# Half 0's second-norm work queued behind the newest output-weight split, and new asking places for norms, loads and the first gate and up weights

## The chip, the cores and the metric

The kernel runs on one core of a Trainium2 chip. The metric is the device time of one execution in microseconds. Before the change it was 1154.78 us, the median of three runs (1154.27 to 1156.89). The execution that was profiled took 1155.71 us; its trace spans 1153.9 us from the first to the last instruction of the program.

## The reference

One decoder layer over 1024 positions of width 1024, in float32:

```python
h = rms_norm(x, ln_pre_mix)
proj = h @ w_in                                   # pool channels, q, k, v
q, k = rope(q, pos), rope(k, pos)
pool_out = multi_scale_pool(u_pool, w_pool, pool_scale)
attn_out = dilated_attention(q, k, v)             # 12 heads, three (window, dilation) settings
mix = concatenate([pool_out, attn_out]) @ w_out
x = x + rms_norm(mix, ln_post_mix)                # "first norm" below
h = rms_norm(x, ln_pre_ffn)                       # "second norm" below
f = (silu(h @ w_gate) * (h @ w_up)) @ w_down
x = x + rms_norm(f, ln_post_ffn)
```

where `rms_norm(x, g)` is `x * rsqrt(mean(x*x) + 1e-6) * g` over the channels.

## The kernel before

**Number format.** Activations and weights lie with channels on the 128 partitions. Every large product is made of three matmuls (`PASSES`, line 256): an operand is split into an upper part, a rounded copy, and a lower part, what is left of it; upper by upper, upper by lower and lower by upper are summed. A weight tile of 128 x 1024 is loaded into a raw tile (`wraw`, three buffers, line 235), its upper part is written by ScalarE (ACT, line 244), its lower part by VectorE (DVE) or GpSimd (POOL, two halves), line 248. `split` and `wtile` (lines 243 to 254) do this; the split tiles named `whl` have two buffers.

**Halves.** The 1024 positions are worked in two halves of 512, half 0 and half 1, written `h`.

**Stages.** Input projection, attention and the pooling mixer take the first part of the span; the output projection of half 0 is woven into the end of attention. Then come, around 440 to 560 us, the output projection of half 1, the two norms of each half, and the first gate and up products. From there on a scheme of seven products per two-by-two block carries gate and up (`seven`, line 1324), and the down projection and the last norm end the kernel.

**Who sets the order.** Matmuls run in the order in which they are written (`keep_in_program_order`). That order is made by hand: `put` (line 952) and `emit` (line 901) give each step of a list a place between a lower and an upper number, sort all steps by place, and run them. In the attention part the unit of place is one of twelve units (head pair and half); some steps also pull filler matmuls until a reckoned due time is reached (`await_`, line 488; the constants `lt`, `ls`, `lm`, `lw`). On the other engines the build's scheduler sets each engine's order from the order of writing and from its own reckoning of when operands are ready, and the engine's queue holds them in that order. `with tc.issue_after(i)` adds, for each instruction traced inside on the engine of `i`, that it must stand behind `i` in that engine's queue; it adds no wait between engines. DMA loads are issued by SyncE's queue (SP), in order.

**Half 1's output projection** (`out_proj`, line 1027) has eight output blocks d0 to d7 of 24 matmuls, 192 in all, which are the unit 0 to 1 of its `emit` (line 1215). The first seven k-tiles of d0, d1 and d2 come first (21 matmuls each), then their last k-tile (3 each), then d3 to d7 whole; banks alternate between `pj` (even d) and `s` (odd d). The weights of block d + 1 are asked at the third k-tile of block d: those of d1 at matmul 6, of d2 at 27, of d4 at 78, d5 at 102, d6 at 126, d7 at 150. d3's are asked ahead of everything, into a buffer of their own (`b`). Lower parts of d0 and d1 go to POOL, the others to DVE (line 1034). The buffer of d6's split tile is that of d4.

**A half's two norms** (`chain`, line 1149) consist of: a load of the residual, the first norm's mean (eight small matmuls with `ones`, then ACT, then POOL's power, lines 1132 to 1140 and 273), its row (four transposes, then ACT into `rb`), eight adds, eight squares, the second norm's mean, its row, and scalings:

- `add` (line 1160): two DVE instructions that make x1 in `z` (lines 1162 and 1163), an upper part by ACT (1164), a lower part by DVE (1165), and a store.
- `square` (1169): an ACT square into one of two strips `p`, and a DVE sum into `sq` (lines 1129 and 1130, shared with the first norm's squares).
- `scale` (1178): one ACT instruction on `z` (1181).

Their places are the ten numbers of `c0` (half 0) and `c1` (half 1): mean, row, adds from and to, squares from and to, second mean, second row, scalings from and to. Half 0's first five lists are emitted with half 1's output projection. All else goes with the next stretch (the `emit` at line 1448), in which one unit is 48 steps of three matmuls: the gate and up products of two feed-forward tiles with half 0, and two products of the seven-scheme. The products of the same two tiles with half 1 follow it from place 1.0, at the same 48 steps to the unit. The second tile's weights are asked there at `ew` (gate, up), and `ahead` makes sums of weight blocks on DVE (lines 1331 to 1337) and splits on POOL (1367).

Of the kernel before, what the change touches and what calls it, by code (L numbers as in the profile page):

```python
# [8 lines left out]
F32 = mybir.dt.float32  # L9
F32R = mybir.dt.float32r  # L10
AF = mybir.ActivationFunctionType
ALU = mybir.AluOpType
# [6 lines left out]
NK = 8  # L19
# [19 lines left out]
 'oq': (0, 1, 1, 1, 0, 0, 0, 1),  # L39
 'lag': 3.0,  # L40
# [109 lines left out]
 'cut': 5,  # L150
 'ew': (0.11, 0.19),
 'c1': (0.08, 0.17, 0.18, 0.8, 0.4, 0.95, 1.57, 1.7, 0.6, 0.94),
 'c2': ((0.95, 1.35), (1.4, 1.6)),
 'e0': ((0.26, 0), (0.42, 0), (0.47, 0.9)),
 'e1': (((1.08, 0), (1.28, 0), (1.3, 1.9)), ((2.0, 0), (2.01, 0), (2.02, 2.03)))}
PRM["x"] = {(0, 'm'): 5, (0, 's', 0): 8, (0, 's', 1): 6, (0, 's', 2): 5, (0, 's', 3): 3, (0, 's', 4): 2, (0, 's', 6): 3,
# [31 lines left out]
def hybrid_block(ctx: ExitStack, tc: tile.TileContext, xT, w_in, w_v, w_pin, w_pool, w_out, w_gate, w_up, w_down,  # L188
                 g1, g2, g3, g4, pscale, cost, sint, maskA, maskB, quadA, quadB, lsel, ident, perm, band, out):
    nc = tc.nc  # L190

    def mm(*a, **k):
        return tc.keep_in_program_order(nc.tensor.matmul(*a, **k))  # L193
# [9 lines left out]
    def did(key):  # L203
        seen[key] = seen.get(key, 0) + 1

    def need(key, n):
        assert seen.get(key, 0) >= n, (key, n, seen.get(key, 0))
# [8 lines left out]
    def bank(tag):  # L216
        return psum.tile([P, 512], F32, name="ps_" + tag, tag=tag)
# [9 lines left out]
    def cload(src, shape, name, pool=None, eng=nc.sync):  # L227
        t = (pool or const).tile(shape, F32, name=name)
        eng.dma_start(t, src)
        return t  # L230

    loads = []

    def raw_tile(src, own=None):
        r = own or wpool.tile([P, 1024], F32, name="wraw", tag="wraw", bufs=3)
# [5 lines left out]
        return r  # L241

    def split(dst, src, eng, pin=lambda x: x):
        nc.scalar.activation(dst[:, 0], src, AF.Copy)  # L244
        n = src.shape[-1]
        w = n if eng is nc.vector else n // 2
        for at in range(0, n, w):
            pin(eng.tensor_tensor(dst[:, 1, at:at + w], src[:, at:at + w], dst[:, 0, at:at + w].bitcast(F32), ALU.subtract))  # L248

    def wtile(src, eng=None, pool=None, tag="whl", bufs=2, raw=None, pin=lambda x: x):  # L250
        r = raw_tile(src, raw)
        w = (pool or wpool).tile([P, 2, 1024], F32R, name=tag, tag=tag, bufs=bufs)
        split(w[:, :, :r.shape[-1]], r, eng or nc.gpsimd, pin)
        return w
# [28 lines left out]
    def slot(k, shape, dt, name):  # L283

        return xgp.tile(shape, dt, name=name, tag="xk%d" % k)
# [119 lines left out]
    ls = [cload(lsel[i], [P, P], "ls%d" % i, con1) for i in range(2)]  # L405
# [616 lines left out]
    def room(h, n):  # L1022
        if h:
            return fw([P, 2, 2, 512], F32R)
        return slot((2, 3, 6, 7)[n], [P, 2, 2, 512], F32R, "m0%d" % n)

    def out_proj(h, parts, done):

        box = {}

        def weights(d):
            if d not in box:
                own = h == 1 and d == 3
                box[d] = wtile(w_out[d], nc.gpsimd if d < 2 else nc.vector,
                               *((xgp, "xk5", 1) if d == 2 else (ffnl, "b4", 1) if own else ()),
                               raw=big(5, [P, 1024], F32, "b5") if own else None)

        def step(d, k, first, last, n):
            if first and n == 0:
                weights(d)  # L1040
                box[d] = box[d], bank("s" if d % 2 else "pj")
            if k == 4 and n == 0 and d + 1 < NK:
                weights(d + 1)
            w, ps = box[d]
            if k < 2:
                need(("pool", h), 2)
            if k == 7:
                need(("v", 5, h), 2 * len(GROUPS[h]))
            mk = m[h][k // 2 - 1 if k > 1 else 3][:, k % 2]
            a, b = PASSES[n]  # L1050
            mm(ps, w[:, a, k * P:(k + 1) * P], mk[:, b], start=(first and n == 0), stop=(last and n == 2))
            if last and n == 2:
                did(("z", h, d))
                nc.scalar.activation(z[h](d), ps, AF.Copy)
                if done:
                    done(d, ps)
        ks = (2, 3, 4, 5, 0, 1, 6, 7)
        order = ([(d, k) for kk in (ks[:7], ks[7:]) for d in range(parts) for k in kk]
                 + [(d, k) for d in range(parts, NK) for k in ks])
        return [lambda a=(d, k, k == ks[0], k == ks[-1], n): step(*a) for d, k in order for n in range(3)], weights  # L1060
# [11 lines left out]
    for step, at in zip(mixed(0), G["lr"]):  # L1072
        put([step], at, 0)
    st, weights = out_proj(0, 3, None)
    for d in range(2):
        put([lambda d=d: weights(d)], G["lw0"][d], 0)
# [72 lines left out]
    def chain(h, sq, s3, at):  # L1149

        sl = slice(h * 512, (h + 1) * 512)
        x = []

        def load():
            for n in range(2):
                x.append(slot((6, 4)[h] + n, [P, 4, 512], F32, "xr%d" % n))
                with tc.issue_after(behind.ins) if h else ExitStack():
                    nc.sync.dma_start(x[n], xT[:, 4 * n:4 * n + 4, sl])

        def add(d):  # L1160
            zd, (hi, lo) = z[h](d), (t[:, d % 4] for t in block(d // 4, h))
            nc.vector.scalar_tensor_tensor(zd, zd, g2s[:, d:d + 1], sq.rb, op0=ALU.mult, op1=ALU.mult)  # L1162
            nc.vector.tensor_tensor(zd, zd, x[d // 4][:, d % 4], ALU.add)  # L1163
            nc.scalar.activation(hi, zd, AF.Copy, scale=g3s[:, d:d + 1])
            nc.vector.scalar_tensor_tensor(lo, zd, g3s[:, d:d + 1], hi.bitcast(F32), op0=ALU.mult, op1=ALU.subtract)
            nc.sync.dma_start(x1d[d, :, sl], zd)
            did(("x1", h, d))

        def square(d):
            need(("x1", h, d), 1)  # L1170
            s3.add(d, z[h](d))
            did(("s3", h, d))

        def rows():
            s3.rows(r3[:, sl])
            did(("r3", h))

        def scale(d):
            need(("s3", h, d), 1)
            did(("g3", h, d))  # L1180
            nc.scalar.activation(z[h](d), z[h](d), AF.Copy, scale=g3s[:, d:d + 1])
        return [([load], -1, 0), ([sq.mean], at[0], 0), ([sq.rows], at[1], 0),
                ([lambda d=d: add(d) for d in range(NK)], at[2], at[3]),
                ([lambda d=d: square(d) for d in range(NK)], at[4], at[5]),
                ([s3.mean], at[6], 0), ([rows], at[7], 0),
                ([lambda d=d: scale(d) for d in range(4 if h else NK)], at[8], at[9])]

    put([next_pools], G["np"], 0)
    sqs = [(Squares(), Squares(tag=("o", "pj")[h], to=eps[:, 4 * h:4 * h + 4])) for h in range(2)]
# [10 lines left out]
    def big(n, shape, dt, name):  # L1200

        return ffnl.tile(shape, dt, name=name, tag="b%d" % n)

    def block(kh, h):

        if (kh, h) not in B:
            n = {(0, 0): 0, (1, 0): 2, (1, 1): 4}.get((kh, h))
            B[kh, h] = [(fw([P, 4, 512], F32R, "fw") if n is None else big(n + i, [P, 4, 512], F32R, "b%d%d" % (kh, h)))
                        for i in range(2)]
        return B[kh, h]  # L1210

    st, weights = out_proj(1, 3, sqs[1][0].add)
    weights(3)
    first_half = chain(0, *sqs[0], G["c0"])
    emit((st, 0.0, 1.0), *first_half[:G["cut"]])
    behind = loads[-2]
# [225 lines left out]
    def next_weights(f, i):  # L1442
        with tc.issue_after(powers[-1].ins):
# [3 lines left out]
    ratio = len(beside) / len(before)  # L1447
    emit((before, 0.0, 1.0), (beside, 1.0, 1.0 + ratio), (one[2], 1.0 + ratio, 1.0 + ratio + len(one[2]) / len(before)),
         *first_half[G["cut"]:], ([lambda: let_go(kept)], G["c0"][7] + 0.001, 0), *chain(1, *sqs[1], G["c1"]),
         *(([lambda a=(f, i): next_weights(*a)], G["ew"][i], 0) for f in range(1, EARLY) for i in range(2)),  # L1450
         ([ahead], 0.1, 0), ([lambda: let_go(held)], G["c1"][7] + 0.001, 0),
# [266 lines left out]
```

## Time and profile before

| What | us |
|---|---|
| median of three runs | 1154.78 |
| profiled execution | 1155.71 |
| span of its trace | 1153.9 |
| PE (matmul) busy | 1128.3 |
| PE weight loads busy | 979.2 |
| DVE busy | 790.1 |
| POOL busy | 604.1 |
| ACT busy | 545.4 |

A row of a timeline gives the start in us from the span's start, the length, engine, line, operation, what is written and read, the shape and the count of merged instructions; the bracket gives the engine's idle time before it and what ended it. A matmul's end is modelled, and matmuls overlap, so a busy PE is not yet a PE at its peak: the distance between the starts of two blocks tells how fast they ran. "Granted clock" is the share of full clock that TensorE was given.

### The profile page before, as it was taken

The page shows a single profiled execution, that of the slowest core. Times are in us where ns is not written, and L with a number is a line of the kernel's source. Part 1 is how long each engine was busy: PE and PEld are TensorE (multiplying, and loading weights), DVE is VectorE, ACT ScalarE, POOL GpSimd, SP SyncE. Part 2 cuts the span into 40 slices and gives each one's busy share as a digit, 9 for nine tenths or more (in the row PEclk, how much of TensorE's full clock was granted, in tenths as well). Part 3 has the DMA queues.
Part 4 walks back from the last instruction along what each step waited for, and adds up shares of the span by engine and source line. Part 5 has one row for each costly group of instructions (what it writes and reads, how often), then busy time and mean ns, then how long its engine had stood idle before and what let it go on. Part 6 is the DMA issues. An engine that isn't in the chain of part 4 may idle for free.

```text
span 1153.9 us, 17223 instructions
## 1 busy us (share of the span) xinstructions
PE 1128.3 (98%) x6134; PEld 979.2 (85%) x6134; DVE 790.1 (68%) x1481; ACT 545.4 (47%) x1035; POOL 604.1 (52%) x541
## 2 busy tenths in 40 slices
PE   9999999999999999899999999999999999999996
PEld 7999999999898888778788888888888888888895
DVE  7957878787788674979467655676556365554685
ACT  7456676665677663855333222322232435443420
POOL 0103646465476222250487656876676978566521
PEclk9999999999999999999999999999999999999998
DMA  8224151515136457430344354545444869666542
GB/s 289 107 78 165 56 165 56 164 57 172 49 119 246 169 217 253 166 110 28 126 155 149 137 199 166 183 154 200 165 178 172 279 228 364 211 218 197 169 146 73
DMA packets 85797, 188.51 MB, mean 163 GB/s; under 512 B 8784, under 2 KB 24656, under 8 KB 84304
## 3 DMA queue, kind: packets, MB, share of 16 engines
q1 hardware_dynamic: 84992, 186.89, 46.7%
q8 instruction: 48, 0.79, 0.3%
q10 hardware_dynamic: 720, 0.53, 0.1%
q14 instruction: 37, 0.30, 0.1%
HBM read 134.44 MB, written 52.95 MB: 162 GB/s over the span
## 4 chain that ended last, share of the span: by engine, by line
PE 80%; DVE 9%; issue 3%; DMA 3%; ACT 2%; POOL 1%; SPq 0%; POOLq 0%; DVEq 0%; ACTq 0%
PE ps_pj L193 28%; PE ps_o L193 22%; PE ps_s L193 20%; PE ps_t L193 7%; PE ps_t L196 3%; DMA wraw<-in_w_out_dram 1%; DVE sq L1130 1%; ACT pp L678 1%; DVE z L1162 1%; DMA b<-in_w_out_dram 1%; DVE z L1163 1%; DVE pp L675 1%; DVE tT L1291 1%; DMA xraw<-in_xT_dram 1%; DMA wraw<-in_w_gate_dram 1%
## 5 line engine op out<-in xcount | busy, mean ns | idle before, releaser
L193 PE MATMUL ps_pj<-x,whl 128*128 128x512 f32 x480 | 143.1, 410 | 0.0
L1367 POOL TENSOR_TENSOR fw<-rw,fw 128x512 fp32r<-128x512 f32 x74 | 101.6, 1398 | 65.2 <-ACT fw L1365 63.8
L248 POOL TENSOR_TENSOR whl<-wraw,whl 128x512 fp32r<-128x512 f32 x50 | 66.6, 1353 | 121.6 <-ACT whl L244 121.6
L193 PE MATMUL ps_o<-tT,fw 128*128 128x512 f32 x504 | 117.7, 389 | 0.0
L193 PEld LDWEIGHTS ps_o<-tT,fw 128*128 128x128 f32 x504 | 94.5, 188 | 19.9 <-DVE sq L1402 0.3
L730 POOL TENSOR_SCALAR pp<-pp,wv 128x256 f32<-128x256 f32 (+1 forms) x156 | 72.8, 486 | 72.4 <-DVE wv L714 63.7
L678 ACT ACTIVATE pp<-pp,sx 128x128 f32<-128x128 f32 (+1 forms) x192 | 89.4, 468 | 34.9 <-DVE sx L675 34.1
L193 PEld LDWEIGHTS ps_pj<-x,whl 128*128 128x128 f32 x480 | 85.7, 191 | 9.4
L1367 POOL TENSOR_TENSOR whl<-rw,whl 128x512 fp32r<-128x512 f32 x42 | 59.9, 1449 | 60.4 <-ACT whl L1365 55.5
L1365 ACT ACTIVATE fw<-rw 128x1024 fp32r<-128x1024 f32 x37 | 38.5, 1056 | 94.3 <-DVE rw L1333 43.0
L193 PE MATMUL ps_pj<-whl,x 128*128 128x256 f32 x528 | 81.0, 293 | 0.0
L1514 POOL TENSOR_TENSOR op<-rw,op 128x512 fp32r<-128x512 f32 x38 | 60.2, 1584 | 37.1 <-ACT op L1513 34.9
L1513 ACT ACTIVATE op<-rw 128x1024 fp32r<-128x1024 f32 x38 | 40.2, 1060 | 65.2 <-PE ps_t L193 30.2
L193 PEld LDWEIGHTS ps_pj<-whl,x 128*128 128x128 f32 x528 | 70.3, 196 | 0.1
L776 DVE TENSOR_TENSOR ptr<-ps_t,ptr 128x512 fp32r<-128x512 f32 (+1 forms) x84 | 55.9, 665 | 16.4 <-ACT ptr L775 15.9
L450 POOL TENSOR_TENSOR rsw<-rsw,sinr 128x512 f32<-128x512 f32 x20 | 26.3, 1316 | 70.9 <-DVE rsw L448 70.9
L193 PE MATMUL ps_pj<-b,fw 128*128 128x512 f32 x264 | 61.6, 389 | 0.0
L775 ACT ACTIVATE ptr<-ps_t 128x512 fp32r<-128x512 f32 (+1 forms) x84 | 48.4, 576 | 23.0 <-PE ps_t L196 22.2
L193 PEld LDWEIGHTS ps_pj<-b,fw 128*128 128x128 f32 x264 | 49.5, 188 | 10.3
L193 PE MATMUL ps_o<-ptr,v 128*128 128x128 f32 (+1 forms) x472 | 56.4, 254 | 1.8 <-DVE ptr L776 1.2
L193 PEld LDWEIGHTS ps_o<-ptr,v 128*128 128x128 f32 x472 | 52.8, 163 | 5.9 <-DVE ptr L776 1.6
L193 PE MATMUL ps_s<-k,qh 128*128 128x128 f32 (+1 forms) x192 | 53.9, 292 | 0.0
(305 smaller groups left out, 2920.5 us busy)
## 6 DMA issues: line engine op xcount, KB each, us to landing
rw<-bd SPq DMA_DIRECT2D x77, 256.0 KB, 4.8
v<-vd SPq DMA_DIRECT2D x22, 512.0 KB, 4.7
rw<-wsd SPq DMA_DIRECT2D x44, 256.0 KB, 3.9
rw<-in_w_gate_dram SPq DMA_DIRECT2D x20, 512.0 KB, 3.6
rw<-in_w_up_dram SPq DMA_DIRECT2D x20, 512.0 KB, 4.7
bd<-p SPq DMA_DIRECT2D x33, 256.0 KB, 2.9
rw<-in_w_down_dram SPq DMA_DIRECT2D x33, 256.0 KB, 4.8
fw<-in_w_down_dram SPq DMA_DIRECT2D x16, 512.0 KB, 4.0
```

Source lines behind the costliest of these rows:

```text
L193: return tc.keep_in_program_order(nc.tensor.matmul(*a, **k))
L196: return tc.keep_in_program_order(nc.tensor.transpose(dst, src, by))
L248: pin(eng.tensor_tensor(dst[:, 1, at:at + w], src[:, at:at + w], dst[:, 0, at:at + w].bitcast(F32), ALU.subtract))
L450: pin(eng[0].tensor_tensor(s, s, sinr[:, sl], ALU.mult))
L678: nc.scalar.activation(pt[:, j, lo:], pt[:, j, lo:], AF.Exp, bias=sx[:, 0, side, j, hd, 0:1], scale=-1.0, accum_out=sx[:, 0, side, j, hd, ...
L730: nc.gpsimd.tensor_scalar(pv, pv, un.wv[:, side, j, hd:hd + 1], 1.0, op0=ALU.mult, op1=ALU.mult)
L775: nc.scalar.activation(ptr[:, 0, :w], t[:, :w], AF.Copy)
L776: nc.vector.tensor_tensor(ptr[:, 1, :w], t[:, :w], ptr[:, 0, :w].bitcast(F32), ALU.subtract)
L1365: nc.scalar.activation(w[n][:, :, 0], raw[n], AF.Copy)
L1367: low[0] = nc.gpsimd.tensor_tensor(w[n][:, i, 1], raw[n][:, i], w[n][:, i, 0].bitcast(F32), ALU.subtract)
L1513: nc.scalar.activation(w[:, :, 0], raw, AF.Copy)
L1514: nc.gpsimd.tensor_tensor(w[:, 0, 1], raw[:, 0], w[:, 0, 0].bitcast(F32), ALU.subtract)
```

## The change

Three things are done.

First, `split` remembers its instructions, and half 1's output projection keeps those of its newest weights in `next_up`: the ACT copy and the last instruction of the lower part. Half 0's adds, squares and scalings are traced behind these two in the queues of their engines.

Second, the places in `c0`, `c1`, `c2` (sums of blocks for the seven-scheme) and `ew` are set anew.

Third, attention's constants are set anew: due times, loads of values (`vt`), places of the pooling products (`pw`, `pm`), of the mixed rows' loads (`lr`, `lc`), of half 0's output weights and projection (`lw0`, `o0` to `o2`) and of its first squares (`z0`, `z1`).

```diff
- 'lt': 2.644,
- 'ls': 2.2,
- 'lm': 2.759,
- 'lw': (3.952, 0.492),
+ 'lt': 2.638,
+ 'ls': 2.287,
+ 'lm': 2.745,
+ 'lw': (4.153, 0.453),
...
- 'f1': -0.003,
+ 'f1': -0.0015,
...
- 'vt': ((1.06, 1.318), (2.8322, 3.3), (4.97, 5.4541), (6.97, 7.1607), (8.9599, 10.177), (9.83, 10.1116)),
- 'pw': 0.45,
- 'pm': (0.92, (0.8357, 0, 0), (0.84, 1, 0), (0.99, 0, 1), (1.05, 1, 1)),
+ 'vt': ((1.06, 1.2775), (2.7383, 3.2225), (4.97, 5.5237), (6.9389, 7.3255), (8.9599, 10.3692), (9.9449, 10.1116)),
+ 'pw': 0.4464,
+ 'pm': (0.8885, (0.7664, 0, 0), (0.84, 1, 0), (0.99, 0, 1), (1.0616, 1, 1)),
...
- 'lr': (9.8566, 10.0981, 9.97, 10.2561),
- 'lw0': (9.9996, 10.2477),
- 'lc': (11.63, 11.6315, 11.66, 12.1584),
- 'o0': 10.4948,
- 'o1': 11.12,
- 'o2': 12.856,
- 'np': 11.62,
- 'z0': 11.9358,
- 'z1': 13.05,
- 'c0': (0.13, 0.2, 0.21, 0.6, 0.3, 0.7, 0.25, 0.42, 0.25, 0.7),
+ 'lr': (9.8605, 9.8142, 9.9709, 10.2193),
+ 'lw0': (9.928, 10.3976),
+ 'lc': (11.9344, 11.9085, 11.9739, 12.2843),
+ 'o0': 10.4915,
+ 'o1': 11.122,
+ 'o2': 12.6068,
+ 'np': 11.6655,
+ 'z0': 12.4302,
+ 'z1': 13.859,
+ 'c0': (0.0502, 0.0986, 0.2259, 0.595, 0.2709, 0.6103, -0.3497, 0.3883, 0.2606, 0.1296),
  'cut': 5,
- 'ew': (0.11, 0.19),
- 'c1': (0.08, 0.17, 0.18, 0.8, 0.4, 0.95, 1.57, 1.7, 0.6, 0.94),
- 'c2': ((0.95, 1.35), (1.4, 1.6)),
+ 'ew': (0.2207, 0.1793),
+ 'c1': (0.1405, 0.1771, 0.2651, 0.7788, 0.6483, 1.0204, 1.4605, 1.6658, 0.9644, 0.8869),
+ 'c2': ((1.0107, 1.1787), (1.1914, 1.4876)),
...
     def split(dst, src, eng, pin=lambda x: x):
-        nc.scalar.activation(dst[:, 0], src, AF.Copy)
+        parts = splits[:] = [nc.scalar.activation(dst[:, 0], src, AF.Copy)]
         n = src.shape[-1]
         w = n if eng is nc.vector else n // 2
         for at in range(0, n, w):
-            pin(eng.tensor_tensor(dst[:, 1, at:at + w], src[:, at:at + w], dst[:, 0, at:at + w].bitcast(F32), ALU.subtract))
+            parts.append(eng.tensor_tensor(dst[:, 1, at:at + w], src[:, at:at + w], dst[:, 0, at:at + w].bitcast(F32), ALU.subtract))
+            pin(parts[-1])
+            splits[1:] = parts[1:]
...
                                raw=big(5, [P, 1024], F32, "b5") if own else None)
+                if h:
+                    next_up[:] = splits
...
+        def queued(f):
+
+            def step():
+                with ExitStack() as s:
+                    for i in (next_up[:1] + next_up[-1:]) if h == 0 else ():
+                        s.enter_context(tc.issue_after(i.ins))
+                    f()
+            return step
         return [([load], -1, 0), ([sq.mean], at[0], 0), ([sq.rows], at[1], 0),
-                ([lambda d=d: add(d) for d in range(NK)], at[2], at[3]),
-                ([lambda d=d: square(d) for d in range(NK)], at[4], at[5]),
+                ([queued(lambda d=d: add(d)) for d in range(NK)], at[2], at[3]),
+                ([queued(lambda d=d: square(d)) for d in range(NK)], at[4], at[5]),
                 ([s3.mean], at[6], 0), ([rows], at[7], 0),
-                ([lambda d=d: scale(d) for d in range(4 if h else NK)], at[8], at[9])]
+                ([queued(lambda d=d: scale(d)) for d in range(4 if h else NK)], at[8], at[9])]
```

More of the change, by code (lines that the diff above doesn't have):

```diff
@@ L230, in cload @@
         return t
-    loads = []
+    loads, splits = [], []
     def raw_tile(src, own=None):
@@ L1025, in room @@
         return slot((2, 3, 6, 7)[n], [P, 2, 2, 512], F32R, "m0%d" % n)
+    next_up = []
     def out_proj(h, parts, done):
```

## The prediction

> **What bounds the kernel now.** I read busy time by stretch first, then who TensorE (PE) waited for, then the timelines of four engines around the longest of those waits. The windows (length, busy time and count of PE, PEld, DVE, ACT, POOL, granted TensorE clock, DMA share, GB/s):
>
> ```profile
> 304.00:308.00 4.00, 4.00 (x16) 3.35 (x14) 3.21 (x7) 1.19 (x2) 4.00 (x9) 0.60 0.00 0
> 363.40:366.00 2.60, 2.60 (x16) 2.60 (x16) 2.49 (x5) 1.50 (x3) 2.60 (x7) 0.65 0.99 377
> 440.00:560.00 120.00, 113.61 (x519) 93.16 (x519) 91.65 (x122) 69.82 (x115) 37.64 (x26) 0.99 0.37 130
> 481.67:488.17 6.50, 6.50 (x23) 5.29 (x23) 6.50 (x9) 4.27 (x7) 0.00 (x0) 0.77 0.25 81
> 560.00:1140.00 580.00, 580.00 (x2694) 485.70 (x2694) 349.07 (x409) 191.34 (x221) 375.20 (x264) 1.00 0.55 191
> ```
>
> From 560 to 1140 us TensorE never pauses, and the diff touches nothing there: half of the span is fixed. In 440 to 560, the stretch of half 1's output projection, the four norms and the first gate and up products, PE is idle 120.00 - 113.61 = 6.4 us. There the change can work directly. The waits:
>
> ```profile
> PE ps_t L196 <- POOL pp L730: 3.1, 3, 1.8
> PE ps_pj L196 <- POOL nrr L273: 3.0, 2, 2.0
> PE ps_pj L193 <- DVE whl L248: 2.9, 1, 2.9
> ```
>
> The longest single wait (2.9) is for a weight split on DVE. PE's timeline shows where it and its neighbours stand; "[idle <- releaser]" closes a row:
>
> ```profile
> 478.12 0.61 PE L193 MATMUL ps_pj<-fw,whl 128*128 128x512 f32 x2
> 481.67 6.66 PE L193 MATMUL ps_pj<-fw,whl 128*128 128x512 f32 x22 [2.94 <-DVE whl L248]
> 488.17 5.60 PE L193 MATMUL ps_s<-fw,whl 128*128 128x512 f32 x24
> 493.61 2.88 PE L193 MATMUL ps_t<-b,whl 128*128 128x512 f32 x12
> 497.95 1.02 PE L193 MATMUL ps_o<-ones,sq 128*128 128x1 f32 x8 [1.46 <-DVE sq L1130]
> ...
> 550.08 0.95 PE L193 MATMUL ps_pj<-ones,sq 128*128 128x1 f32 x8
> ...
> 557.26 0.65 PE L196 MATMUL ps_pj<-idt,nrr 128*128 128x128 f32 x4 [1.98 <-POOL nrr L273]
> ```
>
> A block of 24 matmuls takes 493.61 - 488.17 = 5.44 us, 0.227 each. Block d6 runs two matmuls with the upper part of its weights and then waits 2.94 us for the lower part. Its other 22 then need 6.50 us instead of 4.99, at a granted clock of 0.77: (1 - 0.77) x 6.50 = 1.50 us lost besides. So this one late split costs 2.94 + 1.50 = 4.44 us.
>
> [...]
>
> **Why that split is late.** DVE and ACT around it:
>
> ```profile
> 454.98 1.22 DVE L248 TENSOR_TENSOR b<-b,b 128x1024 fp32r<-128x1024 f32 x1 [6.75 <-ACT b L244]
> 456.12 5.38 DVE L1162 SCALAR_TENSOR_TENSOR z<-z,g2s,rb 128x512 f32<-128x512 f32 x8
> ...
> 468.52 1.40 DVE L1165 SCALAR_TENSOR_TENSOR b<-z,g3s,b 128x512 fp32r<-128x512 f32 x2
> ...
> 471.05 8.23 DVE L1165 SCALAR_TENSOR_TENSOR b<-z,g3s,b 128x512 fp32r<-128x512 f32 x6
> 479.20 1.28 DVE L1130 TENSOR_TENSOR sq<-sq,p 128x512 f32<-128x512 f32 x2
> 480.41 1.21 DVE L248 TENSOR_TENSOR whl<-wraw,whl 128x1024 fp32r<-128x1024 f32 x1
> ...
> 491.04 2.55 DVE L1130 TENSOR_TENSOR sq<-sq,p 128x512 f32<-128x512 f32 x2 [1.87 <-ACT p L1129]
> ...
> 494.65 3.16 DVE L1130 TENSOR_TENSOR sq<-sq,p 128x512 f32<-128x512 f32 x3
> ```
>
> ```profile
> 453.89 1.06 ACT L244 ACTIVATE b<-b 128x1024 fp32r<-128x1024 f32 x1 [3.17 <-DMA b<-in_w_out_dram]
> 454.85 0.58 ACT L1147 ACTIVATE rb<-ps_o 128x512 f32<-128x512 f32 x1
> ...
> 475.79 1.08 ACT L244 ACTIVATE whl<-wraw 128x1024 fp32r<-128x1024 f32 x1
> ...
> 490.90 0.63 ACT L1129 ACTIVATE p<-z 128x512 f32<-128x512 f32 x1
> ```
>
> ACT has d6's upper part at 476.87, DVE makes the lower part only at 480.41, because half 0's adds (L1162 to L1165) and square sums stand before it. That backlog began at 456.12, after DVE had sat 6.75 us behind d3's split, which ACT could not feed until a load landed; the norm row rb followed on ACT right behind the same copy. And POOL:
>
> ```profile
> 469.47 7.93 POOL L1367 TENSOR_TENSOR op<-rw,op 128x512 fp32r<-128x512 f32 x4 [17.65 <-DMA x1d<-z]
> 490.05 3.00 POOL L248 TENSOR_TENSOR whl<-wraw,whl 128x512 fp32r<-128x512 f32 x2 [12.64 <-ACT whl L244]
> ...
> 553.73 2.51 POOL L1367 TENSOR_TENSOR whl<-rw,whl 128x512 fp32r<-128x512 f32 x2 [4.94 <-ACT nrr L268]
> 556.20 1.01 POOL L273 TENSOR_TENSOR nrr<-nrr,half 128x4 f32<-128x4 f32 x1
> ```
>
> **The change part by part.** Positions become matmuls by counting steps: 192 in half 1's projection, 48 steps of three matmuls in the unit after it.
>
> Half 0's first norm (c0, first two): the mean goes from after 25 matmuls to after 10, the row from 39 to 19. The row is thus 20 x 0.227 = 4.5 us earlier. Whether rb is too is not in the trace: if ACT still puts d3's copy before it, DVE starts its adds at 456.12 as now (0 gained); if not, up to 4.5 us earlier. I take half, 2.3. Only 10 matmuls now stand behind the last squares of half 0; the nearest row for a mean asked too soon is the 1.46 above, so 0 to 1.5 us. I take 0, since the projection of half 0 ends 0.25 unit earlier (o2), and the last attention products cover it.
>
> The queueing. Half 0's adds are asked at matmuls 43 to 105 (c0, .2259 to .595), its squares at 52 to 109; d6's split enters at 126. So no add or square can be held behind d6 or d7: the new edges hold adds behind d2, d4 and d5, whose splits PE already finds ready. Only the scalings, now asked in the next stretch, stand behind d7's split. They leave ACT's queue ahead of d6's copy, which is worth little: the copy was done 3.5 us before DVE took it. A held add waits at worst for one DVE split, 1.21 us.
>
> So d6's split moves by the earlier start, 2.3 us: its end from 481.62 to 479.35. PE wants it at 478.57, waits 0.8 instead of 2.94, and keeps its clock (1.50 us is about all the clock that the row of 440 to 560 lacks, 0.01 of 120, so the waits of 1.46 and 1.98 cost none): 2.1 + 1.5 = 3.6 gained. Gate and up start at 490.0 instead of 493.61.
>
> Half 0's second mean: c0[6] goes from .25 to -.3497, ahead of all gate and up matmuls. PE takes matmuls in the order written, so everything in that stretch queues behind eight tiny matmuls that need half 0's last square sum. Its square is the last one from z, at 490.90 on ACT, and its sum is the second of the two at 491.04, so it ends by 493.59. Moved 2.3 us earlier it ends at 491.3, and PE waits 1.3 us. Bounds: 0 (sums 4.5 earlier) and 4.2 (sums behind all others, 497.81). It gives back 1.3; nothing hides it.
>
> Half 1's first mean (c1, .08 to .1405): after 21 matmuls instead of 12, 2.0 us later, against a wait of 1.46: 1.46 gained if half 1's sums come forward with the start, as they stand in the same DVE queue. The row stays after 27, so 6 matmuls (1.4 us) are left between mean and row.
>
> Half 1's second norm: mean after 71 steps (76), row after 80 (82). The mean is 3.4 us earlier and POOL's power at 556.20 no longer stands behind the two splits of 2.51 us; mean to row is 27 matmuls, 6.1 us, instead of 18. The 1.98 goes.
>
> First feed-forward weights (ew): up's second tile is now asked before gate's second tile, which PE needs first. At worst that costs about one split on POOL, 3.00; POOL sat idle 12.64 us ahead of 490.05 and has room for both, I take 0.
>
> Attention (lt, ls, lm, lw, vt, pm, loads): the order of hundreds of small steps shifts by a step or two. I cannot place these waits. Bounds: if the waits for pp (3.1) and the two stretches of low clock, (1 - 0.60) x 4.00 = 1.6 and (1 - 0.65) x 2.60 = 0.9, go, -5.6; one more such wait with its low clock, 1.8 + 1.6, is +3.4. I take 0.
>
> Sum: -3.6 + 1.3 - 1.46 - 1.98 = -5.7. The profiled execution took 1155.71 us (span 1153.9), 0.93 over the median of 1154.78; so 1150.0 in it, and 1149.0 as a median.
>
> **The rivals.**
>
> *The start does not move.* ACT keeps d3's copy before rb, the edges hold nothing that matters, d6 waits as before. Gate and up start at 493.61, when half 0's sums are just done (493.59). Only the two norm waits go: -3.4, 1151.3. For it: d3's load decides, and 3.17 us of ACT idle shows it late.
>
> *The start moves wholly.* d6's wait goes (4.44), the early mean waits for nothing: -7.9, 1146.9; with some attention waits gone as well, down to 1141.3.
>
> *A new attention wait cancels.* -5.7 + 3.4 = -2.3, 1152.5 or a little above. For it: the three waits for pp and the two low clocks show how little slack those steps have. Against it: the due times move by a few per cent only.
>
> *The early mean stops the PE (slower).* If half 0's sums fall behind d7's split and half 1's sums, the last one comes at 497.81 instead of 493.59. With d6 unchanged PE then stands 4.2 us at 493.6, loses the clock (1.5), and gains the 3.44 of the two norm waits: +2.3, 1157.1. It turns slower once the last sum ends later than about 495.6. For it: beside POOL's splits a DVE instruction with two memory inputs takes 1.37 us (471.05) instead of 0.70 (468.52), sums 1.28 (491.04) instead of 0.64 (479.20), and whatever is pushed later meets POOL at 490.05. [...] Against it: the squares are asked 6 to 16 matmuls earlier.
>
> **How the numbers follow.** Forecast 0.36, no moved start 0.18, wholly moved start 0.18, cancelled by attention 0.13, early mean 0.15. 0.2% (2.3 us) is about what a measurement of this kernel can tell from no change. Faster by more: the first three less 0.02, since the second may land inside, 0.70; within: 0.13 + 0.02 + 0.01 of the early mean, 0.16; slower: 0.14. The range leaves out the slower case and the far end of the best one, where attention gains too: 1146.9 less half of 5.6 below, and 1152.5 and somewhat above, so 1144 to 1155.
>
> **What would show it.** Right: a DVE split of d6 that ends within 1 us of PE's need; granted clock 1.00 behind it; the first mean of the gate stretch waiting about 1 us on DVE's sq; no wait of a row for POOL's nrr near 550. Wrong: rb still behind d3's copy; PE idle 3 us or more before the first ps_t; a new wait on pp, ptr or fw with a low clock in attention; PE waiting on the second gate tile.

## The result, and the profile after

The changed kernel takes 1148.61 us (median of 6 runs, 1147.47 to 1149.59); the kernel before took 1155.29 in the same comparison (6 runs, 1154.27 to 1157.20). The ratio is 0.9939, with a 95% interval of 0.9926 to 0.9952: 6.7 us faster. The profiled execution of the changed kernel took 1149.15 us, its span is 1147.4, that is 6.5 less than before. All comparisons below are ratios to runs of the kernel before on the same chip; where two intervals overlap, the order of the two kernels is not shown.

The stretches first. The columns are as in the prediction: length, busy time and count of PE, PEld, DVE, ACT and POOL, granted clock, DMA share, GB/s.

```profile
304.00:308.00 4.00, 4.00 (x15) 3.38 (x15) 3.49 (x7) 1.19 (x2) 4.00 (x10) 0.58 0.00 0
440.00:560.00 120.00, 119.61 (x563) 99.32 (x562) 95.72 (x127) 71.47 (x116) 37.95 (x28) 1.00 0.39 135
475.50:482.00 6.50, 6.50 (x31) 5.37 (x30) 6.50 (x7) 4.65 (x8) 3.04 (x2) 1.00 0.24 81
560.00:1140.00 580.00, 574.72 (x2678) 481.51 (x2676) 346.98 (x411) 190.87 (x221) 375.41 (x263) 1.00 0.54 190
```

Between 440 and 560 us PE is idle 0.39 us where it was idle 6.39. The 6.5 us in which d6 begins (475.50 to 482.00) have the full clock, where 0.77 was granted before. Attention (304 to 308) looks as it did: half 1's projection begins at 443.86 us before and at 443.90 after, so that the attention constants moved nothing up to there, in sum. The last row has less busy time partly because the kernel ends earlier, and partly because of a new wait. Who PE waited for, after:

```profile
PE ps_t L196 <- POOL pp L732: 3.1, 3, 1.8
PE ps_o L193 <- DVE p L1416: 1.6, 1, 1.6
...
PE ps_pj L196 <- POOL nrr L275: 1.0, 1, 1.0
...
PE ps_pj L193 <- ACT q L1409: 0.4, 1, 0.4
```

The 2.9 us for the weight split (DVE whl) is gone, and the 3.0 for the row's power (POOL nrr) is down to one wait of 1.0, at 1137.85, near the kernel's end. New is 1.6 us for a DVE sum at line 1416. PE's timeline after:

```profile
478.09 5.60 PE L193 MATMUL ps_pj<-fw,whl 128*128 128x512 f32 x24
...
488.97 0.95 PE L193 MATMUL ps_o<-ones,sq 128*128 128x1 f32 x8
489.77 5.07 PE L193 MATMUL ps_t<-b,whl 128*128 128x512 f32 x21
494.68 0.95 PE L193 MATMUL ps_o<-ones,sq 128*128 128x1 f32 x8
...
547.91 0.60 PE L196 MATMUL ps_pj<-idt,nrr 128*128 128x128 f32 x4
...
553.81 5.60 PE L193 MATMUL ps_s<-tT,whl 128*128 128x512 f32 x24
559.25 8.32 PE L193 MATMUL ps_o<-tT,fw 128*128 128x512 f32 x36
569.21 3.02 PE L193 MATMUL ps_o<-tT,fw 128*128 128x512 f32 x12 [1.63 <-DVE p L1416]
572.06 3.11 PE L193 MATMUL ps_s<-b,fw 128*128 128x512 f32 x13
```

d6 (478.09) runs whole. Half 0's second mean (488.97), half 1's first mean (494.68) and half 1's second row (547.91) wait for nothing. The two blocks to compare with, before:

```profile
561.86 5.60 PE L193 MATMUL ps_s<-tT,whl 128*128 128x512 f32 x24
...
578.37 4.02 PE L193 MATMUL ps_s<-b,fw 128*128 128x512 f32 x17
```

PE reaches the first of these 561.86 - 553.81 = 8.05 us earlier, and the block behind the new wait 578.37 - 572.06 = 6.31 us earlier. The change gains about 8 us and gives 1.6 of it back.

Where the 8 us come from is seen on ACT, DVE and POOL, after:

```profile
449.90 0.60 ACT L1153 ACTIVATE rb<-ps_o 128x512 f32<-128x512 f32 x1 [2.47 <-PE ps_o L196]
452.28 1.06 ACT L244 ACTIVATE b<-b 128x1024 fp32r<-128x1024 f32 x1 [1.78 <-DMA wraw<-in_w_out_dram]
```

```profile
450.53 2.74 DVE L1168 SCALAR_TENSOR_TENSOR z<-z,g2s,rb 128x512 f32<-128x512 f32 x4 [2.70 <-ACT rb L1153]
...
475.00 1.22 DVE L248 TENSOR_TENSOR whl<-wraw,whl 128x1024 fp32r<-128x1024 f32 x1
...
485.60 0.68 DVE L1136 TENSOR_TENSOR sq<-sq,p 128x512 f32<-128x512 f32 x1
```

```profile
540.52 3.46 POOL L1381 TENSOR_TENSOR whl<-rw,whl 128x512 fp32r<-128x512 f32 x2 [38.16 <-ACT whl L1379]
543.95 1.45 POOL L275 TENSOR_TENSOR nrr<-nrr,half 128x4 f32<-128x4 f32 x1
```

The norm row rb now stands ahead of d3's copy on ACT (449.90 against 452.28), so DVE uses the wait for d3's load to begin half 0's adds, at 450.53 instead of 456.12. d6's split follows at 475.00 instead of 480.41: it is earlier by 5.41 us, nearly all of the 5.59 by which the adds start earlier. POOL makes the row's power at 543.95, right behind one pair of splits.

### The profile page after: what moved, and what is told of

The parts are those of the page before. It is cut to its first block, busy times and chain, and to the rows that moved or that the text cites. A ratio compares the mean times of both kernels' runs of the same rounds, so it can differ in the third digit from the quotient of the medians.

```text
span 1147.4 us, 17220 instructions
## 1 busy us (share of the span) xinstructions
PE 1126.4 (98%) x6134; PEld 978.9 (85%) x6134; DVE 789.6 (69%) x1481; ACT 545.0 (47%) x1035; POOL 603.0 (53%) x541
## 4 chain that ended last, share of the span: by engine, by line
PE 82%; DVE 8%; issue 4%; POOL 3%; ACT 2%; DMA 1%; SPq 0%; DVEq 0%; POOLq 0%; ACTq 0%
PE ps_pj L193 29%; PE ps_o L193 21%; PE ps_s L193 21%; PE ps_t L193 7%; PE ps_t L196 3%; ACT pp L680 1%; DVE sq L1136 1%; DVE pp L677 1%; POOL fw L1381 1%; DMA xraw<-in_xT_dram 1%; POOL whl L1381 1%; POOL whl L248 0%; DVE z L1168 0%; DVE ql L483 0%; DMA rw<-in_w_up_dram 0%
```

## The experiments

Theory A: the gain is that of the early row on ACT (c0[0], c0[1]), which starts DVE's backlog 5.6 us sooner. Its rival: it comes from the queueing. Four kernels take these apart.

**The queueing taken out of the kernel after**

```diff
-                if h:
-                    next_up[:] = splits
```

> The changed kernel without the queueing: half 0's adds, squares and scalings are free of the newest splits; all places stay new. Theory A (the earlier row of half 0's first norm lets DVE start its adds at 450.5 instead of 456.1, and that saves the split of d6): within 1 us of the changed kernel, no wait of PE at d6. Theory B (the queueing saves it): d6 waits again, 3 to 4.4 us slower than the changed kernel.

1149.07 us, ratio 0.9944 (0.9932 to 0.9957), within the interval of the whole change. d6 doesn't wait; d4 does:

```profile
466.39 5.28 PE L193 MATMUL ps_pj<-fw,whl 128*128 128x512 f32 x22 [0.63 <-DVE whl L248]
```

Given the early row, the queueing is worth this 0.63 us in the trace and nothing that the times resolve.

**The queueing alone: the kernel before with the queued steps, all constants old**

> The kernel before with the queueing alone, all places old. Theory A: DVE starts its adds near 456 as before, d6 waits 2 to 3 us, the two norm waits stay: within 1.5 us of the kernel before. Theory B: the wait at d6 and its slow clock go, 3 to 4.4 us faster than before.

1157.86 us, ratio 1.0021 (1.0012 to 1.0030): slower, by 2.2 us in the medians.

```profile
484.15 5.28 PE L193 MATMUL ps_s<-fw,whl 128*128 128x512 f32 x22 [0.50 <-DVE whl L248]
489.27 2.88 PE L193 MATMUL ps_t<-b,whl 128*128 128x512 f32 x12
497.23 1.84 PE L193 MATMUL ps_o<-ones,sq 128*128 128x1 f32 x8 [5.08 <-DVE sq L1136]
```

d6's wait is gone here too, so neither theory holds. The edges did hold adds and sums behind the splits, as DVE's queue shows:

```profile
476.33 1.21 DVE L248 TENSOR_TENSOR whl<-wraw,whl 128x1024 fp32r<-128x1024 f32 x1
...
478.67 1.78 DVE L1171 SCALAR_TENSOR_TENSOR b<-z,g3s,b 128x512 fp32r<-128x512 f32 x1
```

d6's split comes at 476.33 instead of 480.41, ahead of a lower part of an add. But the backlog is only pushed back: it meets half 1's first mean, which now waits 5.08 us instead of 1.46.

**The early row alone: the kernel before with two numbers changed**

```diff
- 'c0': (0.13, 0.2, 0.21, 0.6, 0.3, 0.7, 0.25, 0.42, 0.25, 0.7),
+ 'c0': (0.0502, 0.0986, 0.21, 0.6, 0.3, 0.7, 0.25, 0.42, 0.25, 0.7),
```

> The kernel before with two numbers new: mean and row of half 0's first norm asked after 10 and 19 matmuls instead of 25 and 39. Theory A: rb leaves the copy of d3's weights behind, DVE starts near 450.5, the wait at d6 goes: 3.5 to 5 us faster than before. Theory B: within 1 us of before.

1153.06 us, ratio 0.9974 (0.9963 to 0.9984): faster by 2.6 us in the medians, less than the 3.5 to 5 expected.

```profile
445.18 1.02 PE L193 MATMUL ps_o<-ones,sq 128*128 128x1 f32 x8 [1.33 <-DVE sq L1130]
467.43 5.28 PE L193 MATMUL ps_pj<-fw,whl 128*128 128x512 f32 x22 [0.63 <-DVE whl L248]
493.20 1.02 PE L193 MATMUL ps_o<-ones,sq 128*128 128x1 f32 x8 [1.45 <-DVE sq L1130]
552.52 0.65 PE L196 MATMUL ps_pj<-idt,nrr 128*128 128x128 f32 x4 [1.99 <-POOL nrr L273]
```

d6's 2.94 us are cured by these two numbers alone. What they cost is visible: half 0's first mean comes 1.33 us too soon, and d4 waits 0.63. Both of half 1's waits (1.45, 1.99) stay. In waits that is a net gain of 0.98 us (2.94 less 1.33 and 0.63). The rest of the 2.6 fits the clock that d6's wait no longer lowers (1.00 from 478 to 485 us in this profile, 0.77 from 481.67 to 488.17 before; the mean granted clock is 0.992 over 18 runs of the kernel before and 0.995 over 8 of this one), but no run separates the two.

**The early row with the queueing, nothing else**

> The kernel before, with the early first mean and row of half 0 (c0[0], c0[1]) and the queueing, nothing else. Theory A: the two together cure d6's wait and d4's, and nothing more: half 1's first mean still waits about 1.4 us and its second row about 2.0 us, 1152 to 1153. Rival: once DVE starts early and the splits come first, the backlog is gone and both norm waits go by themselves: 1149.

1152.89 us, ratio 0.9968 (0.9956 to 0.9979): not told apart from the early row alone.

```profile
490.42 0.73 PE L193 MATMUL ps_t<-b,whl 128*128 128x512 f32 x2 [0.53 <-ACT whl L244]
491.83 2.56 PE L193 MATMUL ps_t<-b,whl 128*128 128x512 f32 x10 [0.68 <-POOL whl L248]
512.03 5.32 PE L193 MATMUL ps_s<-b,fw 128*128 128x512 f32 x22 [0.74 <-POOL fw L248]
554.28 0.65 PE L196 MATMUL ps_pj<-idt,nrr 128*128 128x128 f32 x4 [1.94 <-POOL nrr L275]
```

d4's wait is gone, as theory A has it, the 1.33 of half 0's first mean and the row's 1.94 stay. The 1.4 us of half 1's first mean, expected to stay, did not; three small waits of 0.53 to 0.74 for weight tiles came in its place. Theory A holds, and about half of the whole gain is still to be explained by the other constants.

**Attention's constants old in the kernel after** (`lt` to `z1` of the diff)

> The changed kernel with attention's constants (due times, loads, places up to the first squares of half 0) as before; queueing and the late places new. Theory A and B: attention's constants carry nothing, within 1 us of the changed kernel. Rival C: they carry what the late stage does not show, 1.5 us or more slower than the changed kernel, since half 0's projection ends later and its first mean, after 10 matmuls, waits for the last squares (0 to 1.5 us).

1149.56 us, ratio 0.9945 (0.9933 to 0.9958).

```profile
445.27 1.02 PE L193 MATMUL ps_o<-ones,sq 128*128 128x1 f32 x8 [1.33 <-DVE sq L1136]
```

Only one thing comes back: the 1.33 us of half 0's first mean. That is what the new attention constants are there to cover in this profile; the times don't resolve it.

**Half 1's norms: mean, second mean and second row at the old places, in the kernel after**

```diff
- 'c1': (0.1405, 0.1771, 0.2651, 0.7788, 0.6483, 1.0204, 1.4605, 1.6658, 0.9644, 0.8869),
+ 'c1': (0.08, 0.1771, 0.2651, 0.7788, 0.6483, 1.0204, 1.57, 1.7, 0.9644, 0.8869),
```

> The changed kernel with half 1's first mean (.08) and second mean and row (1.57, 1.7) at their old places. Theory D (the new places remove the waits of 1.46 and 1.98 by themselves): 3 to 3.5 us slower than the changed kernel, both waits back. Theory E (the earlier DVE queue would have removed them anyway): within 1 us, no wait of the mean; in the changed kernel the last square sum ends at 493.3, and the mean at its old place would be asked near 492.5, so 0.8 us of wait at most.

1146.54 us, ratio 0.9921 (0.9907 to 0.9936), the lowest ratio of all. Theory D falls: the time did not rise by 3 us.

```profile
492.07 1.02 PE L193 MATMUL ps_o<-ones,sq 128*128 128x1 f32 x8 [0.66 <-DVE sq L1136]
...
548.24 0.65 PE L196 MATMUL ps_pj<-idt,nrr 128*128 128x128 f32 x4
```

Half 1's first mean waits 0.66 us (0 in the kernel after), its second row waits for nothing, and the new 1.63 us at 569 are gone. So the new places of mean and row were not what took the 1.98 us away, and of the 1.46 us they took 0.66; the rest went with the earlier sums.

**Half 0's second mean at its old place (c0[6] .25) in the kernel after**

> The changed kernel with half 0's second mean at its old place, .25, behind 13 steps of gate and up. Theory of the prediction (the early mean costs what half 0's sums are late): in the changed kernel it waits for nothing, so nothing is won: within 0.7 us of the changed kernel. Rival: the early mean pays, since POOL and ACT have it behind them before half 1's work: 1 us or more slower.

1149.01 us, ratio 0.9944 (0.9928 to 0.9959): the early second mean neither costs nor pays. A wait of 2.37 us for a sum of line 1416 stands at 565.56 in its profile, in the place of the 1.63.

**The sums of weight blocks behind the sums that PE waits for, in the kernel after**

```diff
-            nc.vector.tensor_tensor(s3, raw["A11"], raw["A21"], ALU.subtract)
+            with tc.issue_after(u_adds[-1].ins) if j == EARLY // 2 + 1 else ExitStack():
+                nc.vector.tensor_tensor(s3, raw["A11"], raw["A21"], ALU.subtract)
...
-                nc.vector.tensor_tensor(u, ps, t["P1", i], ALU.add)
+                u_adds.append(nc.vector.tensor_tensor(u, ps, t["P1", i], ALU.add))
```

> The changed kernel with one more order on DVE: the first of the block sums for the third pair of feed-forward tiles (j = 2), which waits for a load at 565.95, stands behind the last sum that frees a bank for PE. Theory F (PE's wait of 1.63 at 569.21 is that queueing): the wait goes, 1.5 to 1.8 us faster than the changed kernel. Rival: the load is the limit, and the wait comes back within the next 15 us of PE's time: no gain.

1146.97 us, ratio 0.9926 (0.9911 to 0.9941). The wait at 569 is gone; one of 0.82 us for a sum stands at 603.48 in its place. What made the wait at 569, in the kernel after:

```profile
565.95 2.00 DVE L1345 TENSOR_TENSOR wraw<-rw 128x1024 f32<-128x1024 f32 x1 [2.36 <-DMA rw<-in_w_up_dram]
567.88 0.68 DVE L1387 TENSOR_TENSOR sq<-ps_t,r 128x512 f32<-128x512 f32 x1
568.48 0.68 DVE L1416 TENSOR_TENSOR p<-ps_o,sq 128x512 f32<-128x512 f32 x1
```

DVE stands 2.36 us idle behind a block sum whose raw weights have not landed, and the sum that frees PE's bank (568.48) is queued behind it.

**The same, and the rotary work of attention behind the merge of the softmax parts** (its steps traced behind the merge's exponential on ACT and its last product on DVE)

> As the one before, and the rotary work of attention stands behind the newest merge's exponential on ACT and its last weight on DVE. Theory G (PE's waits at 301 to 304 and at 362, 3.9 us of idle time together, come from rotary work that is queued ahead of the merge): 1.5 to 4 us faster than the one before. Rival: the rotary work then holds its PSUM bank longer and makes waits of the next projection: same or slower.

1154.8 us, ratio 0.9993 (0.9983 to 1.0004): the gain is lost. The waits near 300 to 304 us stay, the one of 1.84 for pp near 361 falls to 0.90, and a large one appears:

```profile
377.25 1.51 PE L193 MATMUL ps_o<-ptr,v 128*128 128x128 f32 x8 [9.80 <-DMA v<-vd]
```

The theory that the rotary work holds these steps up falls for the waits near 301. At 361 the wait is halved, so that there it may be part of the cause; no run tests that alone. What makes these waits, the same in nearly every kernel here, stays open.

**Only half 1's second mean and row at the old places (c1[6] 1.57, c1[7] 1.7), in the kernel after**

> The kernel after, with half 1's second mean and row back at their old places (c1[6] 1.57, c1[7] 1.7); half 1's first mean stays at its new place. Theory H: the wait of 1.63 at 569 us comes from the early second mean: its ACT copy (nrr) stands in ACT's queue ahead of the copies of two weight blocks, holds them for about 2.5 us, so POOL's splits end and the raw weights' load is issued 2.5 us later, and the block sum on DVE with it. With the old place the wait goes although DVE's order of instructions is unchanged, and with the new first mean the 0.66 us wait that stood at 492 goes too: no PE wait over 0.5 us from 440 to 580 us, about 1146.0. Rival: the order on DVE alone makes that wait; it stays at about 1.6, 1148.6.

1148.07 us, ratio 0.9931 (0.9918 to 0.9945), 2.1 us more than expected; in its profile PE waits 0.37 us at 519 and 0.45 for the row, and for nothing at 569. The trace bears theory H out, without a change of DVE's order, though at a smaller size: ACT copies a weight block at 541.64, ahead of nrr's copy, where the kernel after does it behind, at 546.67, and the up weights' second load is issued 0.97 us earlier (560.12 against 561.09) although PE is 0.55 later there, 1.5 us in all where the expectation said 2.5. The time is not told apart from the kernel after.

**In addition half 1's adds at their old places (c1[2:4] .18, .8 instead of .2651, .7788)**

(The "run before last" in the expectation is the kernel just above.)

> The kernel of the run before last with half 1's adds at their old places as well (c1[2:4] .18 to .8 instead of .2651 to .7788). Theory K: what took the row wait away is that these adds are now asked later. With the old places the scheduler puts ten POOL split instructions of about 1.25 us ahead of the small power that the row needs (two before), so the row waits again, 2 to 5 us: 1148 to 1151. Rival: the row wait went because the whole stretch begins earlier; then this run takes the time of the one with only the second mean moved back, within 0.5 us.

1162.6 us, ratio 1.0058 (1.0045 to 1.0071): slower than the kernel before. On PE:

```profile
507.48 1.22 PE L193 MATMUL ps_t<-b,fw 128*128 128x512 f32 x2 [5.69 <-ACT fw L244]
...
561.57 0.65 PE L196 MATMUL ps_pj<-idt,nrr 128*128 128x128 f32 x4 [3.32 <-POOL nrr L275]
```

and on POOL and ACT of the same kernel:

```profile
548.08 5.05 POOL L1381 TENSOR_TENSOR whl<-rw,whl 128x512 fp32r<-128x512 f32 x4 [36.46 <-ACT whl L1379]
553.07 2.55 POOL L1381 TENSOR_TENSOR fw<-wraw,fw 128x512 fp32r<-128x512 f32 x2
555.58 4.97 POOL L1381 TENSOR_TENSOR fw<-rw,fw 128x512 fp32r<-128x512 f32 x4
560.51 1.00 POOL L275 TENSOR_TENSOR nrr<-nrr,half 128x4 f32<-128x4 f32 x1
```

```profile
504.62 0.72 ACT L1170 ACTIVATE fw<-z,g3s 128x512 fp32r<-128x512 f32 x1 [6.98 <-DVE z L1169]
...
506.38 1.04 ACT L244 ACTIVATE fw<-wraw 128x1024 fp32r<-128x1024 f32 x1
```

Theory K is right about the row: its power stands behind ten splits (548.08 to 560.51), and PE waits 3.32 us. It missed the larger cost. Asked earlier, the first upper parts of half 1's adds enter ACT's queue ahead of the copy of gate's second weight tile. ACT stands 6.98 us for DVE's x1, and the copy, which needed nothing from DVE, is made at 506.38; with the adds later, ACT makes it at 497.98. PE waits 5.69 us. This is the price with the new `ew`, which asks that tile later; with the old adds and the old `ew` together, as in the early row with the queueing, the nearest wait is the 0.74 at 512.03.

**In addition to the second mean and row, the first feed-forward weights old (ew .11, .19)**

> The kernel with half 1's second mean and row back at their old places, and the first feed-forward weights too (ew .11, .19). Theory L: their places are worth nothing, PE finds gate's and up's second tiles ready either way: within 0.5 us of the run that has the new ew. Rival: the new order saves a POOL split on PE's path, up to 3.0 us: 1147.5 to 1149.

1147.96 us, ratio 0.9931 (0.9918 to 0.9944), 0.11 us from the kernel with the new `ew`. A row waits 1.80 us for POOL at 497.15, and the small waits at 519 and 549 are gone; in sum the places of `ew` are worth nothing that shows.

Four variants have lower ratios than the change (0.9921, 0.9926 and twice 0.9931 against 0.9939), and in each the trace shows the wait of 1.63 us at 569 gone; all intervals overlap that of the change, so that a better kernel is likely but not shown. The places in `c2`, of half 0's adds, squares, second row and scalings, and of half 1's squares and scalings were never changed alone; what they are worth is not known.

## Why the prediction was right, step by step

The time came out 0.4 us from the forecast; the medians differ by 6.7 us and the spans by 6.5, where the sum said 5.7. Several terms were off, and their errors cancelled, so that the closeness of the number is in part luck. The early start of DVE as the main gain was right, and of the four signs two held: the full clock at d6, and no wait of a row for POOL near 550. The other two did not: d6's split ended at 476.22, 2.3 us ahead of PE's need at 478.54 and not within 1 us of it, and the first mean of the gate stretch waited for nothing.

- *d6's split, -3.6.* Mechanism right, size too small: the row moved ahead of d3's copy, and DVE's start moved wholly (5.59 us, not 2.3). The wait of 2.94 went with its low clock, in this profile 4.44. In the trace this is the rival "the start moves wholly"; its -7.9, with the new waits of 1.63 and 0.39 that it did not foresee, would be -5.9.
- *Half 0's early second mean, +1.3.* Wrong: 0. Half 0's last sum ends at 485.60 + 0.68 = 486.28, and PE asks the mean at 488.97. The prediction moved the sum by 2.3 us from 493.59; it moved by 7.3.
- *Half 1's first mean, -1.46.* Right in size. The place bought 0.66 of it, the earlier sums the rest.
- *Half 1's second row, -1.98.* Right in size, wrong in cause. The kernel with the old mean and row places has no such wait; the one with the old places of half 1's adds has 3.32 us. What counts is where POOL's queue holds the power, and that was set by a constant which the prediction did not look at.
- *The queueing, 0.* Nearly right in size for the changed kernel: it is worth 0.63 us, at d4, whose split PE does not find ready once DVE starts early. It does hold more where the old places stay: alone it took d6's wait away. There the last squares are asked up to place .7, matmul 134, behind d6's weights at 126, and the build's order on DVE put a lower part of an add (478.67) behind d6's split (476.33) as well. The prediction took the asked places for the places on the engine.
- *Half 0's first mean, 0; attention, 0; `ew`, 0.* Right. The cover named for the mean is real: without the new attention constants it waits 1.33 us.
- *Not foreseen: +1.6 at 569 us.* The prediction called 560 to 1140 us untouched. The early second mean of half 1 delays the load of raw weights there, and a block sum that waits for it stands ahead of a sum that PE needs. Running beside it: a wait of 0.39 at 519.58.

Together: 6.38 us of waits less 0.39, and 1.50 of clock, are 7.49 of the 8.05 measured at the block of 553.81; 0.56 is left over. (The low stretch lasts from 481.25 to 484.67; the 3.0 us of it behind d6's wait ran at a clock of 0.50.)

## What to carry to other kernels

An order hint that holds work behind a deadline does not shrink the backlog; it moves it to the next consumer (2.94 us at d6 became 5.08 at a mean). What shrinks it is to start it sooner: here a small row, put ahead of a copy that was waiting for a load anyway, gave some four tenths of the gain with two numbers (0.26% of 0.61%). And when a place is changed, look at which instruction then stands at the head of each in-order queue and what that one waits for: a copy that needed nothing was 8.4 us later because the instruction ahead of it waited for DVE.

## What was not expected of the hardware

The low clock is not a fixed price of a wait. The windows around the same wait for pp, in the kernel after (1.84 us) and in the one without the queueing:

```profile
361.00:368.00 7.00, 6.17 (x36) 6.18 (x37) 5.75 (x11) 2.83 (x7) 7.00 (x13) 0.76 0.99 346
```

```profile
359.00:366.00 7.00, 5.85 (x40) 5.62 (x40) 6.17 (x13) 4.35 (x9) 7.00 (x13) 1.00 0.99 344
```

After it the clock is 0.76 over 7 us in one profile (0.50 from 361.95 to 365.37) and 1.00 in the other. The trace of the kernel before shows the same inside one execution: the wait of 1.84 that ends at 361.55 is followed by 0.50 from 361.79 to 365.20, d6's 2.94 has 0.50 from 481.25 to 484.67, and the row's 1.98 that ends at 557.26 is followed by the full clock (1.00 from 484.70 to 560 and from 560 to 1140). So a longer wait left the clock alone where a shorter one did not.

In the clock records of the kernels before and after, every low stretch ahead of PE's last matmuls is 3.41 us long, at 0.50: three before (from 303.76, 361.79 and 481.25), two after (from 303.93 and 361.95). Inside one execution their starts lie 58.03 and 119.47 us apart before and 58.03 after, that is 17, 35 and 17 of those lengths. What decides whether a wait brings a low stretch is not shown.

So the 1.5 us of clock that the prediction added to d6's wait was real in that profile; that a wait of such a length brings it in every execution is not shown. The starts differ with the low stretches: half 1's projection begins at 443.86 and 443.90 in the kernels before and after, where seven matmuls near 304 take 3.25 and 3.16 us, and at 441.86, 441.39 and 441.48 in the kernel without the queueing, the early row alone and the one with attention's constants old, where the seven take 1.86, 1.85 and 1.86. In the first two of these three the clock near 361 is 1.00 as well.
